# The low halves of 19 weight units made by adding transfers, and softmax weights turned in 64-row pieces

## The chip, the cores and the metric

The kernel runs on one core of a Trainium2 chip. The metric is the device time of one execution in microseconds (us); the time of a kernel is the median of several runs. The core's engines run side by side, each through its own list of instructions in order: TensorE (in the profile PE, its weight loads PEld), VectorE (DVE), ScalarE (ACT), GpSimd (POOL) and SyncE (SP), which starts the transfers from memory. An engine waits on semaphores that other engines or transfers raise.

## The reference

Two layers work on 256 latent tokens and 256 context tokens of 1024 channels. Each layer has a token-mixing part and a channel-mixing part. The token-mixing part, cut to what matters here:

```
h  = modulate(rmsnorm(x, norm1_g), sh1, sc1)        # latents; the same for the context
p  = h @ w_in                                       # one combined projection
p -> p_glu (2*512), q, k, v (3*512), p_gate (2*1024)
y_conv = silu(layernorm(dwconv31(a * sigmoid(g)))) @ w_conv_out     # a, g = split(p_glu)
s_win  = rope(q) . rope(k) * 64**-0.5 + bias        # 8 heads of 64, window keys
s_ctx  = q . k_ctx * 64**-0.5
w      = softmax(concat(s_win, s_ctx))
y_attn = (w_win @ v + w_ctx @ v_ctx) @ w_na_out
x      = x + g1 * ((sig(p_gate1) * y_conv + sig(p_gate2) * y_attn) @ w_out)
```

Context tokens attend only to context tokens. In the second (last) layer only the latents go on after the keys and values. The channel-mixing part is a gated feed-forward block of 2816 channels with a convolution of width 3.

## The kernel before

**Layout.** Channels lie on the 128 partitions, tokens along the free dimension: `LAT` is columns 0 to 255, `CTX` 256 to 511. A weight *unit* is a block of 128 x 1024 float32 (512 KB), that is eight stationary blocks of 128 x 128: one block of 128 output channels.

**High and low parts.** Products run on rounded numbers (`fp32r`) in three passes so that the result keeps float32's accuracy. `wparts` loads a unit into a `raw` buffer by SyncE's queue, ScalarE rounds it into `whi` (`act.copy`, L160), and VectorE subtracts to get what is left, `wlo` (L161). `raw`, `whi` and `wlo` have four buffers each. `mm3` then issues three matmuls: high weights by high activations (L179), high by low (L180), low by high (L181). In the first layer each has 512 columns (latents and context together), in the second mostly 256. `group` runs the eight blocks of a unit and calls `slot()` half-way and at its end.

**Side work.** `slot()` moves each registered generator on by a step: the attention (`Attention.run`), the convolution's taps (`conv_run`, VectorE, L591, two per slot in the first layer), later the layer norm (`layer_norm`, whose first two sums run on GpSimd, L842 and L843), and the modulation vectors. So the order in which each engine gets its work comes from where the slots fall in the sequence of groups; each engine's list is fixed when the program is built.

**The first layer's attention.** After the V products and the first GLU unit pair the order of units is q0, k0, GLU1 a and b, q1, k1, GLU2 a and b, q2, k2, GLU3 a and b, q3, k3, and then gates 0 to 4: these are the 19 units numbered from `U_IN`. They run at about 60 to 200 us of the span. A pair q, k serves two heads. `Attention.step` takes, in this order:

1. `turn`, for the scores taken in the step before: TensorE transposes the softmax weights `pp` (queries on partitions) in blocks of 128 x 128 into PSUM banks (L494 for latents, L499 for context), and ScalarE copies each bank of four blocks into a tile `pT` with keys on partitions (L495, L500).
2. `values`, for what was turned a step earlier: sixteen matmuls of `pT` by `V` into the bank `po` (L512); ScalarE and VectorE then split the result into `oh` and `ol` (L518, L519).
3. `products`, for the next pair: the scores (L440), 64 channels of a head on each half of the rows, the two heads one after the other on alternate halves (`HALF`), into the banks `sc`, `sc`, `pt` and one of `main`; then the softmax (L458 to L482) by VectorE and ScalarE.

There are eight PSUM banks: four `main`, two `sc`, one `pt`, one `po`. Turns and products use the same banks, so the products of a step wait until ScalarE has copied the turned weights out. The first layer has six turns (four of latents, two of context), the second four of latents, with the same code. Sixteen transposes make a turn.

Elsewhere on ScalarE: the GLU's sigmoid (L606), the roped q and k (L768), copies of gates (L628), silu of the modulation vector (L255).

Of the kernel before, what the change touches and what calls it, by code (L numbers as in the profile page):

```python
# [8 lines left out]
F32 = mybir.dt.float32  # L9
F32R = mybir.dt.float32r  # L10
BF16 = mybir.dt.bfloat16
AF = mybir.ActivationFunctionType
ALU = mybir.AluOpType
AX = mybir.AxisListType

P = 128
# [3 lines left out]
S = 256  # L20
# [11 lines left out]
UW = 1024  # L32
LAT, CTX = slice(0, S), slice(S, 2 * S)
# [3 lines left out]

U_GLU0, U_V, U_IN, U_NA, U_CO, U_WO, U_UP, U_DN = 0, 2, 6, 36, 40, 44, 52, 96
NU = 118
T_GLU, T_Q, T_K, T_GATE = 0, 6, 10, 14  # L40

SWAP16 = [(i + 16) % 32 for i in range(32)]
# [3 lines left out]
def trunk(ctx: ExitStack, tc: tile.TileContext, xt, cvec, crow, wall, wada, params, bias_t, rope_t, out):  # L46
    nc = tc.nc
    pe, act, dve, pool, sp = nc.tensor, nc.scalar, nc.vector, nc.gpsimd, nc.sync
# [4 lines left out]
    wp = ctx.enter_context(tc.tile_pool(name="w", bufs=1))  # L53
# [6 lines left out]
    def nm(s):  # L60
        uid[0] += 1
        return f"{s}_{uid[0]}"
# [3 lines left out]
    def psum(tag="main"):  # L66
        return psp.tile([P, 512], F32, tag=tag, bufs=BANKS[tag], name=nm(tag))

    def tmp(w=512):
        return tp.tile([P, w], F32, tag="t", bufs=5, name=nm("t"))  # L70
# [4 lines left out]
    def sl(w, i):  # L75
        return w[:, i * P : (i + 1) * P]
# [29 lines left out]
    start = ExitStack()  # L106
# [5 lines left out]
    ident = cp.tile([P, P], F32, name="ident")  # L112
# [32 lines left out]
    def raw_unit(src, r=None):  # L145
        r = wp.tile([P, UW], F32, tag="raw", bufs=4, name=nm("raw")) if r is None else r
        lastdma[0] = sp.dma_start(r, src)
        return r

    def wparts(l, u, at=None, cuts=2):  # L150

        r = wp.tile([P, UW], F32, tag="raw", bufs=4, name=nm("raw"))
        hi = (at or wp).tile([P, UW], F32R, tag="whi", bufs=4, name=nm("whi"))
        lo = (at or wp).tile([P, UW], F32R, tag="wlo", bufs=4, name=nm("wlo"))
        cs = [slice(i * UW // cuts, (i + 1) * UW // cuts) for i in range(cuts)]
        for c in cs:
            lastdma[0] = sp.dma_start(r[:, c], wall[l, u][:, c])

        def split(c):
            act.copy(hi[:, c], r[:, c])  # L160
            dve.tensor_tensor(lo[:, c], r[:, c], hi[:, c].bitcast(F32), ALU.subtract)  # L161

        def more():
            for c in cs[1:]:
                split(c)

        split(cs[0])
        return (hi, lo), more

    def wunit(l, u, at=None, cuts=1):  # L170
        w, more = wparts(l, u, at, cuts)
        more()
        return w

    def cols(w, i):
        return sl(w[0], i), sl(w[1], i)
# [6 lines left out]
    def group(ps, ws, xh, xl, c):  # L183
# [6 lines left out]
        slot()  # L190
        return ps

    def unit8(l, u, at=None):
        w = wunit(l, u, at)
        return [cols(w, i) for i in range(KD)]


# [185 lines left out]
    HALF = [slice(0, HD), slice(HD, P)]  # L383

    class Attention:
# [99 lines left out]

        def turn(self, what, its, pps):

            pts = [self.eb.tile([P, 4, S], F32, tag="pT", bufs=4, name=nm("pT")) for _ in range(2)]
            for n, tags in enumerate((("sc", "sc"), ("pt", "main"))):
                for i, pp in enumerate(pps[n]):  # L490
                    pt = psum(tags[i])
                    if what == LAT:
                        for kt in range(4):
                            pe.transpose(sl(pt, kt), sl(pp, kt), ident)  # L494
                        act.copy(pts[i][:, :, n * P : (n + 1) * P], pt.rearrange("p (k q) -> p k q", k=4))  # L495
                    else:
                        for t in range(2):
                            for kt in range(2):
                                pe.transpose(pt[:, kt * S + t * P : kt * S + (t + 1) * P], sl(pp, 2 * t + kt), ident)  # L499
                        act.copy(pts[i][:, 2 * n : 2 * n + 2, :], pt.rearrange("p (k q) -> p k q", k=2))  # L500
            js = [its[0][0]] if what == LAT else [it[0] for it in its]
            self.pv.append((what, js, pts))

        def values(self, what, js, pts, bank):
            po = psum(bank)
            kts = range(4) if what == LAT else range(2, 4)
            for n, j in enumerate(js):
                c = slice(n * S, (n + 1) * S)
                for kt in kts:
                    for i in range(2):  # L510
                        h = 2 * j + i
                        pe.matmul(  # L512
                            po[i * HD : (i + 1) * HD, c], self.V[kt][:, h * HD : (h + 1) * HD],
                            pts[i][:, 2 * n + kt - kts[0], :], start=kt == kts[0], stop=kt == kts[-1],
                        )
            for n, j in enumerate(js):
                c = slice(n * S, (n + 1) * S)
                act.copy(self.oh[j][:, what], po[:, c])  # L518
                dve.tensor_tensor(self.ol[j][:, what], po[:, c], self.oh[j][:, what].bitcast(F32), ALU.subtract)  # L519
# [12 lines left out]
    for k in range(KD):  # L532
        sp.dma_start(x[k], xt[k])
        q = tmp()
# [23 lines left out]
    for l in range(DEPTH):  # L558
# [5 lines left out]
        with ExitStack() if last else start as e1a:  # L564
# [49 lines left out]
            def in_group(t, c, tag="main"):  # L614
                return group(psum(tag), unit8(l, U_IN + t), *h1, c)
# [17 lines left out]
            with ExitStack() as e1b:  # L633
# [15 lines left out]
                if l == 0:  # L649
# [27 lines left out]
                    def more():  # L677
                        act.copy(wg[0][:, cuts[0]], rg[:, cuts[0]])
                        act.copy(pb, ps)
                        act.copy(wv[0][:, cuts[1]], rv[:, cuts[1]])  # L680
                        act.copy(wg[0][:, cuts[1]], rg[:, cuts[1]])
                        for w, r, c in ((wv, rv, cuts[0]), (wg, rg, cuts[0]), (wv, rv, cuts[1])):
                            low_part(w, r, c)
# [48 lines left out]
                else:  # L732
                    sp.dma_start(rope, rope_t)
                    pg0 = [psum("sc") for _ in range(2)]
                    for uu in range(2):
                        wg = wunit(l, U_GLU0 + uu)
                        for i in range(2):
                            for kk in range(4):
                                k = 4 * uu + kk
# [59 lines left out]
                n = 0  # L799
# [16 lines left out]
            with ExitStack() as e1c:  # L816
# [71 lines left out]
                for n, pc in branch(U_CO, sh_, sl_):  # L888
                    t = tmp()[:, :T]
# [35 lines left out]
                for n in range(NB):  # L925
                    ps = group(psum(), unit8(l, U_WO + n), *z, ALL)
                    for s in range(NS):
                        residual(sss[s], ps, 2, n, s, s * S)
                    if last:
                        plain(n)  # L930
                    elif n == 0:
                        pace[0] = 0.8
                pace[0] = 0.3
                held = [unit8(l, U_WO + n) for n in range(NB, KD)]
                for s in range(NS if held else 0):
                    for n, w in zip(range(NB, KD), held):
# [13 lines left out]
        with ExitStack() as e2:  # L950
# [45 lines left out]
            if last:  # L996
# [14 lines left out]
                for i, ps in enumerate(pss):  # L1011
                    b = small([P, 1], "wb", 4)
                    act.copy(b, ps[:, S : S + 1])
                    u = ef.tile([P, S], F32, name=f"u{l}_{i}")
# [32 lines left out]
            for i in range(2, KF):  # L1047
                w = [unit8(l, ups[2 * i + t]) for t in range(2)]
# [176 lines left out]
```

## Time and profile before

| | |
|---|---|
| median of 3 runs | 1127.9 us (1127.66 to 1128.62) |
| the profiled execution | 1127.64 us |
| its span, first to last instruction | 1125.9 us |
| TensorE busy | 1114.1 us, 99% |
| VectorE busy | 908.3 us, 81% |
| ScalarE busy | 563.6 us, 50% |
| GpSimd busy | 14.7 us, 1% |
| DMA | 190.83 MB, mean 169 GB/s |

In the profile a row of a group reads: line, engine, operation, output <- inputs, shape, count | busy time in us, mean ns of one | idle time before, with what ended it. A row of the timeline begins with the start and the length in us, and ends in brackets with the idle time before it and its releaser; several alike are one row with their count, whose length runs from the first start to the last end. Matmuls are pipelined: the length of one is longer than its distance from the next. A row of the waits reads: engine and line, what it waited for, us in total, times, longest. A row of windows gives, for a stretch of the span, the busy us and count of PE, PEld, DVE, ACT and POOL, the granted TensorE clock, the DMA share and GB/s.

### The profile page before, as it was taken

The numbers are of one execution on the slowest core, as the hardware profiler recorded it, in microseconds if no ns is written. First come the engines' busy times: TensorE is split into PE (matmuls) and PEld (weight loads), VectorE is DVE, ScalarE is ACT, GpSimd is POOL, SyncE is SP. The second block draws the span as 40 slices with busy tenths as digits, with TensorE's granted clock in tenths as the row PEclk, the third lists the DMA queues.
The fourth block names the chain that finished last, engine by engine and source line by source line (L and its number), as shares of the span: only waits on it lengthen the run. The fifth ranks groups of instructions, "written<-read, shape, count | busy, mean of one in ns | idle before, by whom it ended". The sixth has DMA issues, their size and how long they took to land.

```text
span 1125.9 us, 17731 instructions
## 1 busy us (share of the span) xinstructions
PE 1114.1 (99%) x6828; PEld 963.0 (86%) x6828; DVE 908.3 (81%) x1631; ACT 563.6 (50%) x934; POOL 14.7 (1%) x24
## 2 busy tenths in 40 slices
PE   9999999999999999999999999999999999999997
PEld 7778777787789988888888888989888999999997
DVE  5689999685778788888898555789996898988773
ACT  4347657542333543434343222544677667766642
POOL 0000000000000000000000000000000000000000
PEclk9999999999999999999999999999999999999999
DMA  9833231536734354554556665556433575565781
GB/s 364 282 94 103 75 118 38 206 97 214 245 118 138 114 161 150 168 169 149 168 171 215 219 191 186 180 181 187 145 126 121 167 250 163 188 194 181 219 268 58
DMA packets 53941, 190.83 MB, mean 169 GB/s; under 512 B 6240, under 2 KB 6496, under 8 KB 53856
## 3 DMA queue, kind: packets, MB, share of 16 engines
q1 hardware_dynamic: 53568, 189.65, 52.1%
q8 instruction: 54, 0.88, 0.3%
q14 instruction: 31, 0.25, 0.1%
q10 hardware_dynamic: 288, 0.04, 0.0%
HBM read 188.62 MB, written 1.05 MB: 168 GB/s over the span
## 4 chain that ended last, share of the span: by engine, by line
PE 83%; DVE 9%; issue 6%; ACT 2%; DMA 0%; POOL 0%; POOLq 0%; DVEq 0%; SPq 0%; ACTq 0%
PE main L179 24%; PE main L181 24%; PE main L180 24%; DVE cb L591 4%; PE main L644 4%; DVE wlo L161 1%; PE sc L181 1%; PE sc L179 1%; PE sc L180 1%; PE po L202 1%; PE po L512 1%; PE sc L129 1%; PE sc L440 0%; DMA sb<-in_crow 0%; PE sc L494 0%
## 5 line engine op out<-in xcount | busy, mean ns | idle before, releaser
L179 PE MATMUL main<-h,whi 128*128 128x256 f32 (+1 forms) x1328 | 446.7, 337 | 0.0
L181 PE MATMUL main<-h,wlo 128*128 128x256 f32 (+1 forms) x1328 | 442.9, 335 | 1.0 <-DVE wlo L161 1.0
L180 PE MATMUL main<-h,whi 128*128 128x256 f32 (+1 forms) x1328 | 442.2, 334 | 0.1
L160 ACT CAST whi<-raw 128x1024 fp32r<-128x1024 f32 (+1 forms) x244 | 252.3, 1039 | 285.5 <-PE main L180 131.5
L161 DVE TENSOR_TENSOR wlo<-raw,whi 128x1024 fp32r<-128x1024 f32 (+1 forms) x244 | 292.9, 1207 | 112.5 <-ACT whi L160 108.0
L179 PEld LDWEIGHTS main<-h,whi 128*128 128x128 f32 x1328 | 249.4, 188 | 32.1 <-issue 3.6
L181 PEld LDWEIGHTS main<-h,wlo 128*128 128x128 f32 x1328 | 249.3, 188 | 29.6 <-DVE wlo L161 1.5
L180 PEld LDWEIGHTS main<-h,whi 128*128 128x128 f32 x1328 | 249.8, 188 | 28.5 <-DVE h L367 0.5
L591 DVE SCALAR_TENSOR_TENSOR cb<-u,par,cb 128x512 f32<-128x512 f32 (+1 forms) x240 | 140.4, 609 | 1.4
L271 DVE CUSTOM_DVE_ANT_0 t<-raw,sb,par 128x1024 bf16<-128x1024 f32 x100 | 126.7, 1277 | 1.0 <-ACT sb L255 0.7
L179 PE MATMUL main<-fh,whi 128*128 128x256 f32 (+1 forms) x386 | 123.0, 319 | 0.0
L180 PE MATMUL main<-fl,whi 128*128 128x256 f32 (+1 forms) x386 | 122.9, 319 | 0.0
L181 PE MATMUL main<-fh,wlo 128*128 128x256 f32 (+1 forms) x386 | 122.9, 318 | 0.0
L180 PEld LDWEIGHTS main<-fl,whi 128*128 128x128 f32 x386 | 72.7, 188 | 5.6
L179 PEld LDWEIGHTS main<-fh,whi 128*128 128x128 f32 x386 | 72.7, 188 | 5.6
L181 PEld LDWEIGHTS main<-fh,wlo 128*128 128x128 f32 x386 | 72.7, 188 | 5.5
L963 ACT ACTIVATE t<-main,par 128x512 f32<-128x512 f32 (+1 forms) x82 | 50.6, 667 | 39.0 <-PE main L181 39.0
L964 DVE SCALAR_TENSOR_TENSOR t<-main,par,t 128x510 f32<-128x510 f32 (+1 forms) x82 | 47.5, 615 | 10.2 <-ACT t L963 9.8
L967 DVE SCALAR_TENSOR_TENSOR t<-main,par,t 128x510 f32<-128x510 f32 (+1 forms) x82 | 46.6, 609 | 0.0
L366 ACT ACTIVATE h<-t,mod 128x256 fp32r<-128x256 f32 x56 | 25.4, 502 | 36.1 <-DVE t L365 36.1
L898 DVE SCALAR_TENSOR_TENSOR x<-main,mod,x 128x256 f32<-128x256 f32 x48 | 22.1, 479 | 23.5 <-PE main L181 23.3
L644 PE MATMUL main<-whi,h 128*128 128x512 f32 x128 | 40.6, 402 | 0.1
(221 smaller groups left out, 1188.2 us busy)
## 6 DMA issues: line engine op xcount, KB each, us to landing
raw<-in_wall SPq DMA_DIRECT2D x239, 512.0 KB, 4.2
raw<-in_wada SPq DMA_DIRECT2D x88, 512.0 KB, 4.3
bias<-in_bias_t SPq DMA_DIRECT2D x8, 640.0 KB, 4.8
row<-in_wada SPq DMA_DIRECT2D x8, 512.0 KB, 4.7
sb<-in_crow SPq DMA_DIRECT2D x5, 512.0 KB, 6.0
x<-in_xt SPq DMA_DIRECT2D x8, 256.0 KB, 4.4
raw<-in_wall SPq DMA_DIRECT2D x8, 256.0 KB, 7.1
out<-t SPq DMA_DIRECT2D x3, 256.0 KB, 2.1
```

Of the source, the lines that this page charges most:

```text
L160: act.copy(hi[:, c], r[:, c])
L161: dve.tensor_tensor(lo[:, c], r[:, c], hi[:, c].bitcast(F32), ALU.subtract)
L179: pe.matmul(ps, w[0], xh, start=start, stop=False)
L180: pe.matmul(ps, w[0], xl, start=False, stop=False)
L181: pe.matmul(ps, w[1], xh, start=False, stop=stop)
L271: dve.tensor_tensor_reduce(tmp().bitcast(BF16), r, v, 1.0, pr(l, BADA + n, 1), ALU.mult, ALU.add, mods[l][:, n, s : s + 1])
L366: high = act.activation(hi[:, c], y[:, c], AF.Identity, bias=b)
L591: dve.scalar_tensor_tensor(cb[j], src, w, cb[j], ALU.mult, ALU.add)
L644: mm = pe.matmul(pv[t], h1[n == 1][k][:, c], w[n == 2][:, b], start=k + n == 0, stop=k == KD - 1 and n == 2)
L963: act.activation(c, pv_, AF.Identity, bias=pr(l, FDB + t, 1), scale=w[1])
L964: dve.scalar_tensor_tensor(c[:, :, 1:], pv_[:, :, : S - 1], w[0], c[:, :, 1:], ALU.mult, ALU.add)
L967: dve.scalar_tensor_tensor(c[:, :, : S - 1], pv_[:, :, 1:], w[2], c[:, :, : S - 1], ALU.mult, ALU.add)
```

## The change

**Low parts.** For the 19 units of the first layer from q0 to gate 4, `unit8` calls a new function `wadded`. Load and rounding to `whi` stay. ScalarE then writes the negative of `whi` into `wlo` (`act.mul` by -1), and a transfer of GpSimd's queue adds `raw` to it (`accum_op=add`), so that `wlo` holds raw - high as before. VectorE's subtraction is gone for these units. The scratch room for descriptors of such transfers is set to 1024 bytes. In each engine's list the negating copy follows the rounding of its unit closely, mostly next to it; in the turn near 100 us it stands between the rounding and the copies of the turned weights, and also in the one near 132 us. GpSimd's list has fourteen of the transfers, then the layer norm's first sum, four transfers, its second sum, and the last transfer.

**Turns.** `turn` takes the `pp` tiles in halves of 64 queries: each block of 128 x 128 becomes two transposes of 64 rows, one on each half of the rows, whose 64 columns go to a bank of their own. There are 32 transposes per turn in place of 16, first all of one bank pair (`sc`, `sc`), then all of the other (`pt`, `main`). The copies stay four of 512 columns per turn, now with 64 queries of both heads each, and go into one tile `pT` for both heads (two buffers in place of four of half the size). This holds for both layers, ten turns, so 160 transposes become 320.

```diff
+ADDED = {(0, u) for u in range(U_IN, U_IN + 19)}
...
+    def wadded(l, u):
+
+        r = raw_unit(wall[l, u])
+        hi = wp.tile([P, UW], F32R, tag="whi", bufs=4, name=nm("whi"))
+        lo = wp.tile([P, UW], F32R, tag="wlo", bufs=4, name=nm("wlo"))
+        act.copy(hi, r)
+        act.mul(lo, hi.bitcast(F32), -1.0)
+        pool.dma_start(lo, r, accum_op=ALU.add)
+        return hi, lo
+
     def unit8(l, u, at=None):
-        w = wunit(l, u, at)
+        w = wadded(l, u) if (l, u) in ADDED else wunit(l, u, at)
         return [cols(w, i) for i in range(KD)]
...
         def turn(self, what, its, pps):
 
-            pts = [self.eb.tile([P, 4, S], F32, tag="pT", bufs=4, name=nm("pT")) for _ in range(2)]
+            pT = self.eb.tile([P, 2, 4, S], F32, tag="pT", bufs=2, name=nm("pT"))
             for n, tags in enumerate((("sc", "sc"), ("pt", "main"))):
+                outs = [psum(t).rearrange("p (i s q) -> p i s q", i=2, s=4) for t in tags]
                 for i, pp in enumerate(pps[n]):
-                    pt = psum(tags[i])
+                    for s in range(4):
+                        src = s if what == LAT else s % 2 * 2 + s // 2
+                        for pt, r in zip(outs, HALF):
+                            pe.transpose(pt[:, i, s], sl(pp, src)[r], ident[r, r])
+                for pt, r in zip(outs, HALF):
                     if what == LAT:
-                        for kt in range(4):
-                            pe.transpose(sl(pt, kt), sl(pp, kt), ident)
-                        act.copy(pts[i][:, :, n * P : (n + 1) * P], pt.rearrange("p (k q) -> p k q", k=4))
+                        act.copy(pT[:, :, :, n * P + r.start : n * P + r.stop], pt)
                     else:
-                        for t in range(2):
-                            for kt in range(2):
-                                pe.transpose(pt[:, kt * S + t * P : kt * S + (t + 1) * P], sl(pp, 2 * t + kt), ident)
-                        act.copy(pts[i][:, 2 * n : 2 * n + 2, :], pt.rearrange("p (k q) -> p k q", k=2))
+                        to = pT[:, :, 2 * n : 2 * n + 2].rearrange("p i k (t q) -> p i (k t) q", t=2)
+                        act.copy(to[:, :, :, r], pt)
...
-                            pts[i][:, 2 * n + kt - kts[0], :], start=kt == kts[0], stop=kt == kts[-1],
+                            pT[:, i, 2 * n + kt - kts[0]], start=kt == kts[0], stop=kt == kts[-1],
...
-    nc = bacc.Bacc("TRN2", target_bir_lowering=False, num_devices=1)
+    nc = bacc.Bacc("TRN2", target_bir_lowering=False, num_devices=1, dynamic_dma_scratch_size=1024)
```

More of the change, by code (lines that the diff above doesn't have):

```diff
@@ L486, in turn, with values @@
         def turn(self, what, its, pps):
-            pts = [self.eb.tile([P, 4, S], F32, tag="pT", bufs=4, name=nm("pT")) for _ in range(2)]
+            pT = self.eb.tile([P, 2, 4, S], F32, tag="pT", bufs=2, name=nm("pT"))
             for n, tags in enumerate((("sc", "sc"), ("pt", "main"))):
+                outs = [psum(t).rearrange("p (i s q) -> p i s q", i=2, s=4) for t in tags]
                 for i, pp in enumerate(pps[n]):
-                    pt = psum(tags[i])
+                    for s in range(4):
[3 more added lines that the diff above has]
+                for pt, r in zip(outs, HALF):
                     if what == LAT:
-                        for kt in range(4):
-                            pe.transpose(sl(pt, kt), sl(pp, kt), ident)
-                        act.copy(pts[i][:, :, n * P : (n + 1) * P], pt.rearrange("p (k q) -> p k q", k=4))
-                    else:
-                        for t in range(2):
-                            for kt in range(2):
-                                pe.transpose(pt[:, kt * S + t * P : kt * S + (t + 1) * P], sl(pp, 2 * t + kt), ident)
-                        act.copy(pts[i][:, 2 * n : 2 * n + 2, :], pt.rearrange("p (k q) -> p k q", k=2))
+                        act.copy(pT[:, :, :, n * P + r.start : n * P + r.stop], pt)
+                    else:
+                        to = pT[:, :, 2 * n : 2 * n + 2].rearrange("p i k (t q) -> p i (k t) q", t=2)
+                        act.copy(to[:, :, :, r], pt)
             js = [its[0][0]] if what == LAT else [it[0] for it in its]
-            self.pv.append((what, js, pts))
-        def values(self, what, js, pts, bank):
+            self.pv.append((what, js, pT))
+        def values(self, what, js, pT, bank):
             po = psum(bank)
```

## The prediction

> **What bounds the kernel now.** I read the page's busy shares first, then the busy time by windows for the first layer's attention (60 to 200 us) and TensorE's rows in order of time.
>
> ```profile
> span 1125.9 us, 17731 instructions
> PE 1114.1 (99%) x6828; PEld 963.0 (86%) x6828; DVE 908.3 (81%) x1631; ACT 563.6 (50%) x934; POOL 14.7 (1%) x24
> 60.00:200.00 140.00, 140.00 (x748) 110.40 (x747) 137.75 (x268) 91.54 (x183) 2.99 (x2) 1.00 0.28 86
> 60.04 0.40 PE L180 MATMUL main<-h,whi 128*128 128x512 f32 x1
> 60.27 0.39 PE L181 MATMUL main<-h,wlo 128*128 128x512 f32 x1
> ```
>
> TensorE is busy throughout. In the window's row (PE, PEld, DVE, ACT, POOL, granted clock, DMA share, GB/s) it has all 140 us, at a clock of 1.00. Its dense matmuls start every 0.23 us: a weight unit of 24 takes 5.58. The kernel ends when TensorE has got through its list, so an edit counts only where TensorE's list gets shorter or TensorE has to wait.
>
> VectorE is nearly full there too (137.75 of 140), but TensorE has no hole in that stretch; its first real wait comes behind it:
>
> ```profile
> 209.47 0.44 PE L228 MATMUL pt<-ident,t 128*128 128x128 f32 x2 [0.58 <-ACT t L221]
> ACT L255 <- DMA sb<-in_crow: 3.5, 1, 3.5
> ```
>
> It lasts 0.58 us and is released by ScalarE, which had stood 3.5 us for a load (third row, from the waits). A lighter VectorE does not move that load: I leave it.
>
> **Part 1: the low parts.** 19 subtractions (L161) leave VectorE, at 1.21 us each: 23 us of busy time, whose removal I price at 0 for the end, as TensorE waits for VectorE nowhere in the stage. What VectorE does next, the convolution's taps (L591), moves up by about that much. ScalarE gets 19 negating copies of the size of its L160 casts: 19 x 1.05 = 20 us.
>
> ```profile
> L161 DVE TENSOR_TENSOR wlo<-raw,whi 128x1024 fp32r<-128x1024 f32 x20 | 24.2, 1212 | 3.9 <-PE sc L181 3.2 <-ACT whi L160 0.4 <-PE sc L440 0.3
> L160 ACT CAST whi<-raw 128x1024 fp32r<-128x1024 f32 x22 | 23.0, 1051 | 22.4 <-PE main L180 19.7 <-issue 2.7
> raw<-in_wall SPq DMA_DIRECT2D x239, 512.0 KB, 4.2
> 58.18 1.05 ACT L160 CAST whi<-raw 128x1024 fp32r<-128x1024 f32 x1
> 70.74 0.39 PE L181 MATMUL main<-h,wlo 128*128 128x512 f32 x1
> POOL ss L842 <- DVE cb L591: 135.3, 1, 135.3
> 149.47 1.69 POOL L842 TENSOR_TENSOR ss<-cb,cb 128x512 f32<-128x512 f32 x1 [135.32 <-DVE cb L591]
> 155.00 0.39 PE L181 MATMUL main<-h,wlo 128*128 128x512 f32 x1
> ```
>
> ScalarE is busy 91.5 of 140 us, so 111 with the copies: covered, except in front of a turn (below). Each L160 cast ran as soon as TensorE freed its buffer (19.7 us of waits for main L180), three units ahead of its use. The tightest unit is cast at 58.18 to 59.23; with a copy of 0.6 between (an estimate from the kind of copies around it), its negating copy ends by 60.9, and its first low matmul is at 70.74. So the added transfer may take 10 us. No adding transfer stands in this trace; the nearest is a unit's load of the same 512 KB, 4.2 us from issue to landing. I take up to twice that and price it at 0: its cover is the buffers' lead, and without it TensorE waits us for us. SyncE's next load into that `raw` now waits for the transfer instead of the subtraction; four buffers and a DMA share of 0.28 cover this.
>
> POOL's queue has the layer norm's first sum (L842), which waited 135.3 us for the taps, behind the 14th transfer; the 15th, gate 0's, stands behind it. Unmoved it would end at 151.2, and 4.2 us later, at 155.4, the transfer would just miss its use at 155.00. With 14 x 1.21 = 17 us less on VectorE, L842 starts near 133: cover enough, 0.
>
> **Part 2: the turns.** Ten turns (six in the first layer, four in the second) of 16 transposes of 128 x 128 become 32 of 64 rows, in pairs on the two row halves. Today:
>
> ```profile
> 100.45 0.39 PE L181 MATMUL main<-h,wlo 128*128 128x512 f32 x1
> 100.68 1.04 PE L494 MATMUL sc<-ident,pp 128*128 128x128 f32 x8
> 101.55 0.60 PE L494 MATMUL pt<-ident,pp 128*128 128x128 f32 x4
> 102.52 1.16 PE L440 MATMUL sc<-qk,qk 64*128 64x512 f32 x6
> ...
> 132.40 1.04 PE L499 MATMUL sc<-ident,pp 128*128 128x128 f32 x8
> 134.24 1.95 PE L512 MATMUL po<-pT,V 128*64 128x256 f32 x16
> 136.12 0.96 PE L440 MATMUL sc<-qk,qk 64*128 64x512 f32 x6
> L180 PE MATMUL main<-h,whi 128*128 128x512 f32 x624 | 245.3, 393 | 0.0
> L180 PE MATMUL main<-h,whi 128*128 128x256 f32 x688 | 192.4, 281 | 0.1
> L494 PE MATMUL sc<-ident,pp 128*128 128x128 f32 x64 | 8.3, 273 | 0.0
> L494 PEld LDWEIGHTS sc<-ident,pp 128*128 128x128 f32 x64 | 7.4, 141 | 0.8
> L440 PEld LDWEIGHTS sc<-qk,qk 64*128 64x128 f32 x72 | 6.0, 185 | 3.8 <-issue 1.8 <-ACT g L628 1.2 <-ACT pT L495 0.4
> L336 PEld LDWEIGHTS pt<-one,ss 128*128 128x128 f32 x32 | 4.2, 190 | 0.4 <-DVE ss L322 0.3
> L512 PEld LDWEIGHTS po<-pT,V 128*64 128x64 f32 x144 | 9.5, 136 | 5.4 <-issue 1.3
> ```
>
> From 100.68 to 101.55 eight transposes start: 0.109 us each, 1.74 a turn. What sets 0.109? Dense matmuls grow by (393 - 281)/256 = 0.44 ns a column, so one of 128 columns should last 225 ns; a transpose's 273 is 48 more: it streams 128 columns in 56 + 48 = 104 ns, its own spacing. That is a stream bound, and 64 columns would take half, 0.054. The load could bound instead. Plain loads take 190 ns for 128 columns and 136 for 64, 0.84 ns a column on a constant of 82; the transposes' load, 141, is 59 above it. So a pair costs 0.059, if its halves run together. Row halves do so in the score products:
>
> ```profile
> 181.21 0.28 PE L440 MATMUL pt<-qk,qk 64*128 64x256 f32 x1
> 181.21 0.28 PE L440 MATMUL main<-qk,qk 64*128 64x256 f32 x1
> ...
> 81.90 0.40 PE L181 MATMUL main<-h,wlo 128*128 128x512 f32 x1
> 82.23 0.97 PE L440 MATMUL sc<-qk,qk 64*128 64x512 f32 x6
> ```
>
> Both start at 181.21. The bounds for a pair: 0.054 below, and above 2 x 0.059 = 0.118, if the halves take turns. I take 0.059, nearest the kernel's only row-half pairs; 0.109, load or issue bound, stays as the other end of weight.
>
> The Trainium skill ("TensorE: Matmul & The Clock Gate", LDWEIGHTS) says that a load takes its columns divided by 1.2 ns whatever its rows: 107 for 128, near today's 0.109. By it 16 pairs would cost 1.71 and the turn would gain nothing. The trace agrees that 64 rows make a load no shorter (L440's 185 against L336's 190), yet differs in that a transposing load is 49 ns shorter than a plain one of as many columns.
>
> One T-V-P block (132.40): transposes 16 x (0.109 - 0.059) = -0.80. But going from dense matmuls to row halves costs 0.10 more than staying dense (81.90 to 82.23: 0.33 against 0.23), and today's first transpose follows without it. The sixteen values last 1.95 in all and the last some 0.39 of it, so they start every 1.56 / 15 = 0.104; up to the products 1.88 - 16 x 0.104 = 0.21 goes by in changing over. I take that 0.21 for row halves to values too, in place of today's 1.84 - 1.74 = 0.10: +0.11. Net -0.59. Seven turns have this form (132, 160, 177 and 190 us, and three of the second layer's four): -4.1.
>
> The other three are bounded by ScalarE's copies of the turned weights, which free the banks of the products:
>
> ```profile
> 100.65 1.05 ACT L160 CAST whi<-raw 128x1024 fp32r<-128x1024 f32 x1 [2.31 <-PE main L180]
> 101.60 1.06 ACT L495 COPY pT<-sc 128x512 f32<-128x512 f32 x2
> ...
> 111.02 1.28 ACT L606 ACT_TABLE_LOAD   x1
> 112.81 1.07 ACT L495 COPY pT<-sc 128x512 f32<-128x512 f32 x2
> 810.71 1.06 ACT L495 COPY pT<-sc 128x512 f32<-128x512 f32 x2
> 811.63 1.16 PE L440 MATMUL sc<-qk,qk 64*128 64x512 f32 x6
> ```
>
> At 100.68 the cast and the two copies end at 102.66, just behind the products' start at 102.52. The written order puts a unit's negating copy between: the copies end at 103.7, and what of the products needs those banks is 1.2 late; the products that go into `main` come first and fill some 0.4 of it: +0.8. (At 132 a negating copy stands there too, but the values lie between and cover it.) At 110 a table load and a sigmoid hold the copies to 113.9; little of the 0.59 is left: -0.3. At 810 the copies end at 811.77 either way: 0.
>
> Sum: -4.1 + 0.8 - 0.3 = -3.6 against the profiled execution's 1127.64, which stands 0.26 under the median of the three runs: **1124.0 us**.
>
> **The rivals.**
> - *The turn is not cheaper* (0.109 a pair). For it: sixteen loads of 128 columns remain in each half, and half the rows did not shorten L440's. Against: the transpose's stream of 104 ns fills its spacing by itself. Then the seven blocks lose the changes, 7 x 0.21 = +1.5, with 100's +0.8 and 110's +0.1: +2.4, so 1130.0; with halves taking turns (0.118) another 10 x 16 x 0.009 = 1.4, 1131.4. It decides from 0.09 a pair, where seven blocks save only the 0.7 that is lost elsewhere.
> - *Partly*: 0.08 a pair saves 0.46, net -0.25 in seven blocks, -1.8 + 0.8 - 0.1 = -1.1: 1126.5.
> - *The transfers come late* (slower). They run one behind the other on POOL's queue. With 10 us of lead, 19 of them have 150 us, 7.9 each: at 8.5 they need 161.5, and TensorE waits 11.5 at L181: 1135.6. It decides from about 8.1. For it: VectorE's 98% and no row for an adding transfer; against: the 4.2 of a load and a DMA share of 0.28.
> - *More gain*: switches at 0 and no loss at 100: 7 x -0.80 - 0.3 = -5.9, near 1121.7.
>
> The Trainium skill ("SBUF — State Buffer", SBUF: two separate sides) warns that GpSimd cannot write a transfer's descriptors while a two-port mode of VectorE holds the port they share. That would bring the third rival on; no run here shows it, and with the 98% its chance stays at one in ten.
>
> **How the numbers follow.** Forecast 0.48, not cheaper 0.20, partly 0.17, transfers late 0.10, more gain 0.05. The likeliest alone spans 1122.5 to 1125.6; the range, 1121.8 to 1130.8, takes in all but the late transfers and half of the turn-taking end. A measurement tells 0.2% from no change, 2.3 us: under 1125.6 is faster (forecast with a small part off, more gain), above 1130.2 slower (late transfers, half of "not cheaper"): 0.51, 0.27, 0.22.
>
> **What would show it.** A turn's 32 transposes in about 0.95 us, pairs starting together; values 0.23 behind them; products near 100 waiting for ScalarE's copies; no wait of L181's on a transfer; VectorE some 22 us lighter over 60 to 200; L842 near 133. It is wrong if pairs stand 0.1 apart, if a POOL transfer lands after more than 8 us, or if TensorE waits for low parts.

## The result and the profile after

The changed kernel takes 1130.09 us (median of 18 runs, 1128.46 to 1130.6), the kernel before in the same session 1127.87: a ratio of 1.0017, 95% interval 1.0010 to 1.0025. The forecast was 1124.0, with a range from 1121.8 to 1130.8: a fall was forecast, and the time rose. The profiled execution has a span of 1128.0 us, 2.1 more than before.

The page's head, the transfers of GpSimd's queue (size, median us from issue to landing) and the windows of the first layer's attention and of its end, in the columns explained above:

```profile
span 1128.0 us, 18104 instructions
PE 1112.6 (99%) x6988; PEld 956.9 (85%) x6988; DVE 892.7 (79%) x1612; ACT 581.4 (52%) x953; POOL 31.2 (3%) x43
wlo<-raw POOLq DMA_DIRECT2D x19, 512.0 KB, 5.8
60.00:200.00 140.00, 136.50 (x823) 105.18 (x822) 128.11 (x256) 103.77 (x195) 17.47 (x19) 0.99 0.62 152
193.90:197.30 3.40, 3.37 (x26) 2.04 (x26) 0.00 (x0) 3.37 (x6) 0.00 (x0) 0.50 0.00 0
```

TensorE, which had all 140 us of that stretch before, is busy in 136.5: there are holes now, and for 3.4 us behind 193.9 its clock is half. The adding transfers are not what it waits for: they land after 5.8 us in the median, and no row of the waits puts a low matmul of the 19 units down to one.

From the timeline of the same profile, the turn near 100 us (TensorE, then ScalarE) and the last context turn, and one row of the waits:

```profile
101.05 0.71 PE L506 MATMUL sc<-ident,pp 64*128 64x64 f32 x16
101.60 0.22 PE L506 MATMUL pt<-ident,pp 64*128 64x64 f32 x1
101.61 0.22 PE L506 MATMUL main<-ident,pp 64*128 64x64 f32 x1
101.66 0.22 PE L506 MATMUL pt<-ident,pp 64*128 64x64 f32 x1
102.07 0.71 PE L451 MATMUL main<-qk,qk 64*128 64x512 f32 x2
103.59 1.22 PE L451 MATMUL sc<-qk,qk 64*128 64x512 f32 x5 [0.81 <-ACT pT L509]
105.45 0.50 PE L180 MATMUL main<-h,whi 128*128 128x512 f32 x1
...
100.92 1.05 ACT L199 CAST whi<-raw 128x1024 fp32r<-128x1024 f32 x1 [1.94 <-PE main L181]
102.00 1.06 ACT L200 ACTIVATE wlo<-whi 128x1024 fp32r<-128x1024 f32 x1
102.97 1.06 ACT L509 COPY pT<-sc 128x512 f32<-128x512 f32 x2
...
190.74 0.78 PE L506 MATMUL sc<-ident,pp 64*128 64x64 f32 x16
193.34 0.28 PE L506 MATMUL pt<-ident,pp 64*128 64x64 f32 x1 [1.82 <-ACT pp L493]
195.04 3.04 PE L524 MATMUL po<-pT,V 128*64 128x256 f32 x16
198.01 0.50 PE L180 MATMUL main<-h,whi 128*128 128x512 f32 x1
ACT pp L488 <- DVE mx L483: 5.8, 1, 5.8
```

Pairs of transposes start together (101.60 and 101.61) and 0.06 apart: the turn itself is as cheap as forecast. At 100 us the negating copy (L200) stands ahead of the copies of the turned weights, and the products, but for the two that go into `main`, wait 0.81 us for these. At 190.74 the second half of the turn waits 1.82 us for its softmax weights; ScalarE had waited 5.8 us for VectorE's reduction (last row, from the waits). Behind that wait the values take 3.04 us instead of 1.95, inside the window of half clock.

To see where the time went, I take the start of the first dense matmul behind each attention block, less the same in the kernel before; the change of that shift from block to block is what the block cost. At 132 us: 137.70 before and 138.26 after is a shift of 0.56; behind the block before it was 116.70 - 115.55 = 1.15; so the block gave -0.59. All blocks, in us, for the runs that follow too. Each column is one profiled execution; that of add_only is the shortest of its eleven, 1.1 us below their median. Two stretches are left out: the one ahead of 84 us, which differs from the kernel before by -0.2 to +0.6 in these executions, and the one behind the second layer's last values, by -0.9 to +0.2.

| block | forecast | after | turn_only | add_only | late_taps | best12 | add_best12 |
|---|---|---|---|---|---|---|---|
| 100 | +0.8 | +0.88 | 0.00 | 0.00 | +0.88 | +0.01 | -0.01 |
| 110 | -0.3 | 0.00 | +0.57 | +0.11 | +0.01 | +0.01 | -0.01 |
| 132 | -0.59 | -0.59 | -0.59 | -0.01 | -0.60 | -0.60 | 0.00 |
| 160 | -0.59 | -0.60 | -0.59 | 0.00 | +0.35 | +0.33 | 0.00 |
| 177 | -0.59 | +0.21 | -0.59 | +0.01 | -0.58 | -0.59 | 0.00 |
| 190 | -0.59 | +3.64 | +1.61 | +2.34 | -0.61 | -0.61 | 0.00 |
| 200 to 798 | 0 | -0.74 | +0.99 | -0.57 | +1.33 | -0.77 | -0.74 |
| second layer, four turns | -1.8 | -0.78 | -0.81 | 0.00 | -0.73 | -0.80 | -0.02 |
| its last values | 0 | +0.76 | +0.74 | 0.00 | +0.76 | +0.01 | +0.01 |

One block, the last context turn at 190 us, costs 3.64 us; all the other rows together give 0.86.

### The profile page after: what moved, and what is told of

It reads as the page before. It is cut to its first block, busy times and chain, and to the rows that moved or that the text cites. A ratio compares the mean times of both kernels' runs of the same rounds, so it can differ in the third digit from the quotient of the medians.

```text
span 1128.0 us, 18104 instructions
## 1 busy us (share of the span) xinstructions
PE 1112.6 (99%) x6988; PEld 956.9 (85%) x6988; DVE 892.7 (79%) x1612; ACT 581.4 (52%) x953; POOL 31.2 (3%) x43
## 4 chain that ended last, share of the span: by engine, by line
PE 77%; DVE 16%; ACT 4%; issue 1%; DMA 1%; SPq 0%; DVEq 0%; ACTq 0%
PE main L180 23%; PE main L182 23%; PE main L181 23%; DVE cb L603 7%; DVE wlo L162 3%; PE main L656 2%; PE sc L180 1%; PE sc L182 1%; PE sc L181 1%; ACT pp L472 1%; PE po L213 1%; ACT whi L161 1%; ACT pp L475 1%; DVE qk L781 1%; DVE sc L469 0%
## 5 line engine op out<-in xcount | busy, mean ns | idle before, releaser
L161 ACT CAST whi<-raw 128x1024 fp32r<-128x1024 f32 (+1 forms) x225 | 232.4, 1038 | 261.6 <-DMA raw<-in_wall 127.4
L162 DVE TENSOR_TENSOR wlo<-raw,whi 128x1024 fp32r<-128x1024 f32 (+1 forms) x225 | 270.3, 1207 | 116.7 <-ACT whi L161 110.2
L603 DVE SCALAR_TENSOR_TENSOR cb<-u,par,cb 128x512 f32<-128x512 f32 (+1 forms) x240 | 144.9, 621 | 2.6
```

Source lines behind the costliest of these rows:

```text
L603: dve.scalar_tensor_tensor(cb[j], src, w, cb[j], ALU.mult, ALU.add)
```

## The experiments

**First question: does the turn or do the adding units bring the waits, and through what?** My theory after the result ("lists"): the units' edit reorders VectorE's and ScalarE's lists. With 19 subtractions gone, VectorE's list has 120 taps of the convolution ahead of the last context softmax's reduction, where it had 101. Rivals: the new turn itself is to blame; or transfers and GpSimd slow VectorE.

Run turn_only, the new turn with all low parts by VectorE:

```diff
-ADDED = {(0, u) for u in range(U_IN, U_IN + 19)}
+ADDED = set()
```

> The new turn alone, all low parts by VectorE as before. Theory 'lists': the turn's saving is real (a pair of transposes stands 0.061 us apart in the changed kernel), and what ate it are waits that come from the reordered lists of VectorE and ScalarE, which the adding units brought. Then the four blocks at 132, 160, 177 and 190 us each gain 0.59, the one at 110 some 0.3, the one at 100 nothing, the second layer's five together nothing: -2.4 to -2.8, so 1125.1 to 1125.5, and TensorE waits nowhere at the last context turn. Rival 'turn': the smaller transposes themselves bring the waits or let the clock drop; then the loss stays and the time is 1129 or more.

Measured: 1129.18 us, ratio 1.0010 (1.0002 to 1.0019). Timeline of TensorE at the last context turn:

```profile
189.98 0.71 PE L506 MATMUL sc<-ident,pp 64*128 64x64 f32 x16
191.82 0.28 PE L506 MATMUL pt<-ident,pp 64*128 64x64 f32 x1 [1.12 <-ACT pp L493]
193.34 1.95 PE L524 MATMUL po<-pT,V 128*64 128x256 f32 x16
```

Neither theory fits. The time is the one that the rival named, but three blocks gain exactly the 0.59, so the turn's saving is real; yet the wait at 190 is there without any adding unit. TensorE comes to this turn 0.5 us earlier than in the kernel before (189.98 for 190.49), and VectorE comes to the softmax's reduction 1.9 us later (185.32 for 183.39). By the start times in VectorE's timeline, 0.6 of this is there already at its first tap, and 1.2 is the taps ahead of the reduction, 102 for 101. (The +0.99 after 200 us is the wait near 209 for the load of the modulation vector, 1.5 us in this execution and 0.6 in that of before.)

Run add_only, the 19 adding units with the old turn (shortened, against the changed kernel):

```diff
-pT = self.eb.tile([P, 2, 4, S], F32, tag="pT", bufs=2, name=nm("pT"))
+pts = [self.eb.tile([P, 4, S], F32, tag="pT", bufs=4, name=nm("pT")) for _ in range(2)]
...
+                        pe.transpose(sl(pt, kt), sl(pp, kt), ident)
...
```

> The 19 adding units alone, with the old turn of 128 x 128 transposes. Theory 'lists': VectorE's list runs the convolution's taps ahead of the last softmax as in the changed kernel (120 taps stand before its reduction, 101 before the change), so the last context turn waits some 3 us for its softmax weights, the turn near 177 about 0.8, and the one near 100 about 0.9 for the negating copy: 1127.9 + 4.5, so 1132 to 1133.5. Rival 'turn': the adding units are harmless, and the time is 1127.5 to 1128.5.

Measured: 1129.59 us, ratio 1.0013 (1.0004 to 1.0021). TensorE at the last context turn, and ScalarE's negating copy near 100 us:

```profile
190.40 1.04 PE L510 MATMUL sc<-ident,pp 128*128 128x128 f32 x8
193.03 0.83 PE L510 MATMUL pt<-ident,pp 128*128 128x128 f32 x4 [1.59 <-ACT pp L493]
194.58 1.95 PE L523 MATMUL po<-pT,V 128*64 128x256 f32 x16
...
103.32 1.09 ACT L200 ACTIVATE wlo<-whi 128x1024 fp32r<-128x1024 f32 x1
```

The adding units alone bring the wait too (block +2.34), but the time is 2.4 us below the least that I expected: the blocks near 100 and 177 lose nothing. Here the negating copy near 100 stands behind the copies (103.32); it is ahead of them only when both parts are in. So each part makes a wait at 190 by itself: add_only by a later reduction alone (186.52 for 183.39, while TensorE arrives at 190.40 for 190.49), turn_only by a later reduction and an earlier TensorE together.

Run taps_behind, the changed kernel with part of the taps held:

```diff
                         if taps:
-                            conv_tap(*taps.pop(0))
+                            with tc.issue_after(reduced[0].ins) if l == 0 and reduced[0] else ExitStack():
+                                conv_tap(*taps.pop(0))
...
-                dve.tensor_reduce(mx, ps.rearrange("p (q k) -> p q k", q=2), AX.X, ALU.max, negate=True)
+                reduced[0] = dve.tensor_reduce(mx, ps.rearrange("p (q k) -> p q k", q=2), AX.X, ALU.max, negate=True)
```

> The changed kernel with one thing undone: the first layer's taps that the program writes after a context softmax's reductions stay behind them in VectorE's list (99 taps before the last reduction instead of 120). Theory 'lists': the last context turn no longer waits (its block took 3.64 us more than before; it should take 0.6 less), the clock stays full there, and the turn near 177 gains some 0.8: 1130.1 - 4.2 - 0.8 = 1125.1, 1124.5 to 1126.5. Rival 'port': VectorE is late because the transfers and GpSimd slow it, not because of its order; then the last turn still waits for a microsecond or more, and the time is 1129 or more.

Measured: 1128.43 us, ratio 1.0001 (0.9992 to 1.0010). The wait at 190 us shrank but stayed, at 1.1 us. It did not tell the theories apart: this edit holds only the taps of one generator, and 99 still stood ahead of the reduction, nearly the 101 of before.

Run filler, for the half clock: ten products of no use between the halves of the last context turn (shortened).

```diff
+                if n == 0 and what == CTX and self.l == 0 and not self.todo:
+                    fill = psum("po")
+                    with tc.issue_after(tr.ins):
+                        for _ in range(NFILL):
+                            tr = pe.matmul(sl(fill, 0), ident, ident, start=True, stop=True)
```

> The changed kernel with ten products of no use (identity by identity into the idle bank for values) put between the two halves of the last context turn, where TensorE waits 1.8 us. If the half clock for 3.4 us behind that wait comes from TensorE standing idle, the clock stays full, the values there take 1.95 us again instead of 3.04, and the time falls by about 1.1 to 1.5: 1128.6 to 1129.0. If the clock drops for another reason, or the fill itself delays the turn, the time stays at 1130 or rises by up to 1.

Measured: 1129.34 us, ratio 1.0009 (1.0000 to 1.0018).

```profile
190.43 0.78 PE L508 MATMUL sc<-ident,pp 64*128 64x64 f32 x16
191.14 2.50 PE L514 MATMUL po<-ident 128*128 128x128 f32 x20
194.55 1.95 PE L532 MATMUL po<-pT,V 128*64 128x256 f32 x16
```

The values take 1.95 again, the block +2.36 instead of +3.64: with TensorE kept busy through the wait, the clock stays. Standing still for 1.8 us cost another 1.3 us behind it. (The profile has two records for each of these ten products, so x20.) The time fell by 0.75 us, less than the 1.1 expected: the next values cost 0.8 more. The other executions agree: the mean granted clock is 0.996 in twelve of the changed kernel's eighteen and 0.997 or 0.998 in all eleven of the filler. Three of the changed kernel's have 0.998, and these take 1128.46 to 1128.84 us, less than the filler's median; so the half clock doesn't seem to come every time.

**Second question: is the wait VectorE's backlog, or the softmax's own length?** All taps are now held that the program writes after a context softmax's reductions, the layer norm's too, in `conv_tap` itself:

```diff
                 else:
-                    dve.scalar_tensor_tensor(cb[j], src, w, cb[j], ALU.mult, ALU.add)
+                    with tc.issue_after(reduced[-1].ins) if l == 0 and reduced else ExitStack():
+                        dve.scalar_tensor_tensor(cb[j], src, w, cb[j], ALU.mult, ALU.add)
...
+                if self.l == 0:
+                    reduced.append(red)
```

Run late_taps has this edit on the changed kernel.

> The changed kernel with every tap of the first layer that the program writes after a context softmax's reductions held behind them in VectorE's list, those of the layer norm's part too: 83 taps stand before the last reduction, for 120 in the changed kernel and 99 in the run that held only part of them. Theory 'backlog': the last context turn waits because VectorE reaches its reduction late; then it waits no more, its block gains 0.6 instead of losing 3.6, the turn near 177 gains 0.6 as well, and the time is 1125 to 1126. Theory 'chain': what remained of the wait in the run that held part (1.3 us) is the softmax's own length on ScalarE; then 1 us or more of it stays, and the time is 1127.5 to 1128.5.

Measured: 1128.01 us, ratio 1.0001 (0.9992 to 1.0010). TensorE near 190 and, from the waits, what it waits for later:

```profile
191.11 0.71 PE L509 MATMUL sc<-ident,pp 64*128 64x64 f32 x16
192.25 1.95 PE L527 MATMUL po<-pT,V 128*64 128x256 f32 x16
PE po L863 <- DVE ss L860: 1.0, 1, 1.0
PE po L362 <- POOL rs L357: 0.6, 1, 0.6
```

The backlog it is: with 83 taps ahead the reduction starts at 181.94, and the blocks at 177 and 190 give -0.58 and -0.61, what a block gave elsewhere (0.59). But the time fell by 2.1 us and not by 4 to 5: the held taps make the layer norm late, which now holds TensorE near 228 and 240 us (+1.33 in the table), and the block at 160 lost 0.95 against the changed kernel. VectorE has two deadlines.

Run turn_late has the same edit on turn_only.

> The new turn alone, all low parts by VectorE, with the taps held as well: 83 taps before the last reduction, for 102 in the run of the new turn alone. Theory 'backlog': the wait of 1.35 us that the new turn alone had at the last context turn goes, and the time falls from 1129.2 to 1126.5 to 1127.3. Theory 'chain': the wait stays and the time is 1128.5 or more.

Measured: 1127.31 us, ratio 0.9995 (0.9986 to 1.0003), at the upper end of what "backlog" said: the block at 190 gives -0.61 instead of +1.61, and the same two waits for the layer norm appear.

Run before_late has it on the kernel before.

> The kernel before with the taps held, 83 before the last reduction for 101. Theory 'backlog': TensorE waits for no softmax there to begin with, so nothing is gained: 1127.5 to 1128.5, the same as before; if TensorE's list had hidden waits of that kind already, it would be 1 us faster or more.

Measured: 1129.77 us, ratio 1.0020 (1.0011 to 1.0029). A miss: nothing was gained, but 1.9 was lost. The layer norm is late here too, by the waits:

```profile
PE po L351 <- POOL rs L346: 0.8, 1, 0.8
PE main L181 <- DVE wlo L161: 0.5, 1, 0.5
```

and the block at 110 cost 0.79 more. (The profiled execution, 1131.47 us, is 1.7 above the median.) So for the kernel before this order is worse than its own; no other was tried there.

**Third question: can both deadlines be met, and is the turn's gain then as forecast?** Run tidy is late_taps with two more orders of ScalarE's: the negating copy near 100 behind the turn's copies, and the sigmoids of the gates behind the last turn's copies.

```diff
-        act.mul(lo, hi.bitcast(F32), -1.0)
+        with tc.issue_after(turned[0].ins) if u == U_IN + T_GLU + 4 else ExitStack():
+            act.mul(lo, hi.bitcast(F32), -1.0)
...
-                with tc.issue_after(att.exp.ins):
+                with tc.issue_after(turned[-1].ins):
                     for g in raw_gates:
```

> As the run with all taps held, and two things of ScalarE's list besides: the negating copy of the unit near 100 us goes behind the turn's copies, and the gates' sigmoids go behind the last turn's copies in both layers. Theory 'lists': 0.9 more at the turn near 100 (its products no longer wait 1.0 us for the copies) and 0.7 more at the second layer's last values, which waited for VectorE's split of the values before: 1123.5 to 1124.5. Rival: the waits come back in other places of the lists, and the time is that of the run with the taps held alone.

Measured: 1127.35 us, ratio 0.9996 (0.9987 to 1.0004). Both orders did their part: the block near 100 costs 0 (+0.88 before), the last values of the second layer 0 (+0.76). But one microsecond came back elsewhere, as the rival said: the stretch from 200 to 798 us costs +2.34, where late_taps had +1.33. The level was missed by 3 us, mainly because I had taken late_taps at its expected 1125 to 1126.

Runs best12 and best8 let twelve and eight of the held taps go ahead of the last reduction (shortened):

```diff
+                    if l == 0 and len(reduced) == 8 and free[0]:
+                        free[0] -= 1
+                        back = reduced[3]
+                    else:
+                        back = reduced[-1] if reduced else None
```

> The changed kernel with the three orders of the run 'tidy', but twelve of the held taps let go ahead of the last reduction: 95 stand before it instead of 83. Theory 'backlog': VectorE has two deadlines, the last context softmax near 182 us and the layer norm near 227 us; in 'tidy' the first is met and the second is missed, by 1.3 us at the mean's product and about 2 us in all by 250 us. Twelve taps are 8 us of VectorE, so both should be met: no wait at the last context turn, and 1.0 to 1.5 less than tidy's 1127.35, 1125.9 to 1126.4. If one deadline can only be met at the other's cost, the time stays at 1127 or more.

> The same with eight taps let go, 91 before the last reduction. Theory 'backlog': the last context turn has more room, the layer norm 2.6 us less; 1125.9 to 1126.9. Against twelve it tells which of the two deadlines is the tighter.

Measured: **1124.29 us**, ratio 0.9969 (0.9958 to 0.9981), with twelve, and 1124.33, ratio 0.9970 (0.9959 to 0.9982), with eight. Both beat both kernels, by more than expected: I had added up tidy's waits singly, but its whole stretch from 200 to 798 us costs +2.34 by the measure of the table, and best12's gives -0.77. The two times agree, so which of the two deadlines is the tighter stays open. Best12's window, its softmax reduction on VectorE and its turn:

```profile
60.00:200.00 140.00, 139.01 (x850) 107.37 (x850) 119.31 (x245) 107.97 (x201) 18.19 (x19) 1.00 0.63 156
181.43 1.28 DVE L488 TENSOR_REDUCE mx<-sc 128x2 f32<-128x512 f32 x2
189.96 0.71 PE L513 MATMUL sc<-ident,pp 64*128 64x64 f32 x16
191.10 1.95 PE L532 MATMUL po<-pT,V 128*64 128x256 f32 x16
```

The reduction starts at 181.43, right behind the products (186.83 in the changed kernel); the turn waits for nothing, and no wait for the layer norm is left. What is left is at 160 (+0.33): the products there wait 0.36 us for ScalarE's copies, which stand in its list behind a roped q that came late from VectorE.

Run turnbest8 asks whether the turn can have this without the adding units: the new turn alone, eight taps let go, the sigmoids' order.

> The new turn alone, low parts by VectorE, with the taps held but for some six (89 before the last reduction, 32 subtractions among them) and the sigmoids behind the last turn's copies. Theory 'backlog': the last values' wait in the second layer goes (0.7), and the layer norm comes some 4 us earlier than with the taps all held, which takes most of the 2 us of its waits: 1125.3 to 1126.5. If the last context turn waits again by a microsecond, VectorE with all its subtractions can't meet both deadlines, and the time is 1127 or more; then the adding units are what makes room for it.

Measured: 1127.06 us, ratio 0.9991 (0.9982 to 1.0000). The last values and the layer norm were mended, but the block at 190 costs +0.43 again and the one at 110 +0.78. With its 32 subtractions ahead of the reduction VectorE meets one deadline in turn_late and the other here, and not both; numbers of taps between these two were not tried. As far as these runs go, the adding units make the room.

Run add_best12 is best12 with the old turn.

> The run 'best12' with the old turn of 128 x 128 transposes: the adding units and the same three orders, so that the difference to its 1124.29 is the new turn's own worth once nothing waits. By the steps of best12's profile the blocks at 132, 177 and 190 us and two of the second layer gain 0.6 each and one 0.3, the one at 160 loses 0.3: 3.0 us less work for the new turn. Theory 'backlog' gives 1127.0 to 1127.6 for this run, the kernel before less its wait of 0.7 near 209 us. If the orders and the lighter VectorE bring the gain by themselves, it is 1125 or less.

Measured: 1126.63 us, ratio 0.9991 (0.9982 to 1.0000), 0.4 below the range expected. Its attention blocks cost 0.00 against the kernel before, and the stretch after 200 us gives -0.74, the wait near 209 that the kernel before had. Best12 is 2.34 us below it; best12's blocks sum to -0.60 + 0.33 - 0.59 - 0.61 - 0.80 = -2.27. That is the new turn's worth, measured in two ways, and 0.7 less than the 3.0 expected: in the second layer one block gives 0.6, not two.

## Why the prediction was wrong

**Right.** The price of a pair: 0.061 measured (101.60 to 101.66), 0.059 forecast. The changes between row halves and the rest: the blocks at 132 and 160 gave -0.59 and -0.60, forecast -0.59. The negating copy near 100: +0.88 for +0.8. The second layer's first turn: +0.08 for 0. The low parts: transfers landed in 5.8 us in the median and 8.2 at the longest (the one issued at 103.47), which is above the 8 named as a sign of being wrong but below the 10 that the buffers' lead allows, and no low matmul waited for it; GpSimd's first layer-norm sum came at 131.2 for the forecast 133. With other lists the kernel reaches 1124.3, beside the forecast 1124.0, but that they agree so closely is luck: of best12's 3.6 us its attention blocks give 2.3, the wait near 209, which the forecast had left in place, 0.8, and the rest lies in the stretches that the table leaves out.

**The step that failed** is the price of 0 for VectorE's relief, "as TensorE waits for VectorE nowhere in the stage", together with the -0.59 for the blocks at 177 and 190. That TensorE never waited did not mean that its inputs could come much earlier. The rows of the kernel before show by how much they were ahead:

```profile
189.30 1.72 ACT L482 ACTIVATE pp<-pp,ri 128x256 f32<-128x256 f32 x4
190.49 1.03 PE L499 MATMUL sc<-ident,pp 128*128 128x128 f32 x8
191.36 0.60 PE L499 MATMUL pt<-ident,pp 128*128 128x128 f32 x4
191.80 0.60 PE L499 MATMUL main<-ident,pp 128*128 128x128 f32 x4
```

The first row is four pieces of softmax weights, one every 0.40 us, and a transpose waits for its own piece only: in the changed kernel the pieces end at 193.29, 193.68, 194.08 and 194.48, and their first transposes start at 193.34, 193.74, 194.13 and 194.53. In the kernel before the last piece ends at 191.02, and its first transpose, the third of those into `main`, starts at 192.01: 1.0 us of slack. The new turn gets to that piece 0.86 us behind its start, where the old one took 1.52, which leaves 0.33; and three cheaper blocks bring TensorE 1.8 us earlier. Unless the weights came earlier as well, this block could not give the 0.59. VectorE, 98% busy, sets when they come: it was a second bound, 1.0 us behind the first, and I had written its 98% down as harmless.

Nor did the relief help. I had said that the taps move up, and not asked ahead of what. They went ahead of the softmax's reduction. Rows of the changed kernel, and the same reduction in the kernel before:

```profile
182.46 1.22 DVE L162 TENSOR_TENSOR wlo<-raw,whi 128x1024 fp32r<-128x1024 f32 x1
183.59 2.32 DVE L603 SCALAR_TENSOR_TENSOR cb<-u,par,cb 128x512 f32<-128x512 f32 x3
185.83 0.42 DVE L531 TENSOR_TENSOR ol<-po,oh 128x256 fp32r<-128x256 f32 x1
186.17 0.74 DVE L603 SCALAR_TENSOR_TENSOR cb<-u,par,cb 128x512 f32<-128x512 f32 x1
186.83 1.28 DVE L483 TENSOR_REDUCE mx<-sc 128x2 f32<-128x512 f32 x2
...
183.39 1.27 DVE L472 TENSOR_REDUCE mx<-sc 128x2 f32<-128x512 f32 x2
```

The products were done near 182; the reduction ran at 186.83, in the kernel before at 183.39. By the start times in VectorE's timeline, from its first tap to this reduction, the subtractions fall from 17 to 2 and save 17.0 us; but the taps rise from 101 to 120 and take 18.7 us more, and VectorE idles 1.5 us more. Its busy time fell by 9.6 us over 60 to 200 (137.75 to 128.11), where 22 was forecast: six more taps fall into that stretch, and the taps are slower on average (last section), so that taps are busy 9.6 us longer there. That holding taps back is enough to bring the reduction early is shown by late_taps (181.94) and turn_late (180.53). At 177 us the same lateness came by way of ScalarE: behind late softmax weights its copies of the turned weights start at 179.42, for 177.60 in the kernel before, and the products wait 0.23 us for them.

**Terms that were off.** The block at 110 gave 0 for -0.3. In the second layer one of the three blocks gave -0.30 and one +0.03 (its copies come behind a q that waits for VectorE); its last values cost +0.76, which I had not listed: the gates' sigmoids stood ahead of the copy that frees `po`, as tidy shows. The wait of 0.58 at 209 us, left at 0, vanished in the changed kernel, because TensorE came later than the load: -0.7. In best12 it vanished because the load's second transfer landed at 203.07, for 207.01 in the kernel before.

**The rivals.** The measured 1130.09 is the 1130.0 of "not cheaper", by coincidence: the turn was cheaper. "Transfers late" did not happen. What happened, late softmax weights, was not among them. The Trainium skill ("TensorE: Matmul & The Clock Gate", LDWEIGHTS) would have given 1.71 us for the sixteen pairs; they took 1.0, so the measurement decides against that rule for transposing loads.

## What to carry to other kernels

An engine that never waits says nothing on how much earlier its inputs could be there: before pricing a saving on the bound, look at each of its next inputs for when it was ready and when it was taken, and cap the gain with the smallest difference. Time freed on an engine goes to whatever its list can bring forward, and that can be the wrong work; ask what is now ahead of the deadline, and hold it back as far as, and no further than, its own deadline allows (95 taps ahead of the softmax instead of 83 were worth 3 us here).

## What the runs showed of the hardware

Taps that follow each other on the same tile start 0.79 us apart, taps on alternating tiles 0.66 (which tile each works on is read from the program's list, as the rows leave buffer numbers out). Rows of the kernel before and of the changed kernel:

```profile
174.62 6.04 DVE L591 SCALAR_TENSOR_TENSOR cb<-u,par,cb 128x512 f32<-128x512 f32 x9
```

```profile
75.46 8.62 DVE L603 SCALAR_TENSOR_TENSOR cb<-u,par,cb 128x512 f32<-128x512 f32 x11
L603 DVE SCALAR_TENSOR_TENSOR cb<-u,par,cb x120: 732/751/1661, 64.3 to 191.8; 128x512 f32<-128x512 f32 x120
```

Nine start every (6.04 - 0.74) / 8 = 0.66, eleven every (8.62 - 0.75) / 10 = 0.79. In VectorE's list of the kernel before, 6 taps ahead of the last reduction follow one on the same group of channels, 54 in the changed kernel: 48 x 0.13 = 6 us of the relief went there. The two longest taps, 1661 ns (third row: shortest, median and longest in ns) and 1.46 us, stand beside GpSimd's two sums at 131.2 and 160.7; beside the adding transfers none is stretched.

A wait of 1.8 us of TensorE, with small transposes on both sides, was enough for 3.4 us at half clock; from the end of the last dense product (190.8) to the drop (193.9) TensorE had only this wait and transposes, for 3.1 us. Waits of 1.6 us (add_only) and 1.1 us (turn_only) in the same place brought none in their profiled executions. But five of add_only's eleven executions have a mean granted clock of 0.996, as the changed kernel's profiled one has, and take 1129.84 to 1131.1 us; the other six have 0.997 or 0.998 and take 1128.51 to 1129.59. So a wait of 1.6 us may bring it too; where in those five the clock fell is not on record. The Trainium skill ("TensorE: Matmul & The Clock Gate", HAM oscillation — how this bites in real kernels) tells of idle gaps above some 3.4 us as what lowers the clock; the wait that brought it here was shorter.
